# A hybrid attention and RWKV block: a PSUM set of its own for the first stage, five result places, three Newton steps

## The chip, the cores and the metric

The kernel runs on one core of a Trainium2 chip. The metric is the device time of one execution in microseconds (us). Five engines matter: PE (TensorE, matrix multiplication into the accumulator memory PSUM), DVE (VectorE), ACT (ScalarE), POOL (GpSimd) and SP, which issues nearly all transfers (DMA). Each engine runs its own instructions strictly in the order in which they stand, and waits for others through semaphores.

## What is computed

One layer of a sequence model on 1024 tokens with 16 learned tokens ahead of them (1040 columns), width 1024. Cut to what matters here:

```python
hn = rms_norm(h, norm_mix)                 # first stage, by columns
proj = hn @ w_in                           # q, k, v, f_logit, rw, gates
log_f = log_sigmoid(f_logit + f_b)
fcum = cumsum(log_f)                       # "forget": bias of the attention
z = rw + mu * (rw_prev - rw)               # token shift
r, kr, vr, zw, za, zg = split(z)
w_log = -softplus(-(w0 + tanh(zw) @ w_up)) - 0.5
a_rate = sigmoid(a0 + za @ a_up)           # low-rank products: w_up, a_up, g_up
g = sigmoid(zg) @ g_up
...                                        # attention, RWKV scan, gates, w_out
h = h + mixer(...)
h = h + conv_ffn(rms_norm(h, norm_ffn))    # feed-forward, the larger half of the time
```

## The kernel before

Every large product is made of three fp32r matmuls, high times high, high times low and low times high (lines 218, 219, 220), where `wh`, `wl` are the two parts of a weight and `xh`, `xl` those of the normalized input. A projection of one block of 128 output rows over one column chunk is 8 times 3 = 24 matmuls.

The first stage (`stage0`) goes over three column chunks, 0 to 384, 384 to 768, and 768 to 1040. In each, `stats` squares the input (ACT), adds (DVE) and takes column means on PE (line 624) in `rsqrt_rows`; there DVE makes an inverse root by Newton steps of three instructions each (lines 632 to 634), and PE spreads it over the partitions (line 639). `norm` multiplies it in (DVE, line 154, `xt`), rounds (ACT, line 156, `xh`) and takes the rest (line 158, `xl`, on POOL and DVE in turn). `lora` then makes two projections with token shift, `sg` and `wa` (24 matmuls each, evicted by ACT at line 268 and DVE at line 269), and from them twelve low-rank products (line 173): four times a trio of two on 64 rows from `wa` and one on 128 rows from `sg`. ACT evicts each product into a place `o` (lines 176 and 178), POOL scales one of three (line 180), and SP stores it (line 181) to `tha_d`, `sw_d` or `g_d`. The stage ends with the load of another ACT function table (line 191).

After it, several streams run side by side: `att` begins with `forget`, whose 48 matmuls (line 580) in three groups of 16 give the forget logits; a chain on ACT and DVE then makes their running sums, stores them to `f_d`, and POOL's queue loads them into `k2` (line 699) for the attention. `rec` begins with `prep`, which projects K, R and V for four pairs of heads (`zk`, `zr`, `zv`; `proj`, line 347; again 24 matmuls a chunk).

What order each engine has is not written by hand. All streams are recorded, and a scheduler that estimates times puts every engine's instructions into an order when the program is built. It knows the dependences, among them those that come from shared buffers: a PSUM accumulator can't be written before its earlier content is evicted, and a pool of PSUM can't be opened over space that another pool holds.

PSUM accumulators are named by a role, and a table gives the places that a role goes through in turn: A, B, t, o are single banks, S and M two banks each, used as two halves. In the first stage of before it reads:

```python
    banks(S, mm="S S M M", st="t o", pr="A B", t="t", o="o")
```

So projections of the first stage (role `mm`) use halves of S and M, statistics (`st`) use t and o, and the low-rank products use A and B, under the role `pr`, which `prep`'s projections have as well. The matmuls of `forget` use S and M again.

Of the kernel before, what the change touches and what calls it, by code (L numbers as in the profile page):

```python
# [14 lines left out]
PSUM = bass.MemoryType.PSUM  # L15
# [40 lines left out]
def constants(S):  # L56

    nc, A, cp = S.nc, S.A, S.cp
    par = cp.tile([P, NPAR], F32, name="par")
    nc.sync.dma_start(out=par[:], in_=A["par"])  # L60
    S.par = lambda name, i=0: par[:, _PCOLS[name][0] + i:_PCOLS[name][0] + i + 1]
    S.pr = lambda name: par[:, _PCOLS[name][0]:_PCOLS[name][0] + _PCOLS[name][1]]
    S.ident = cp.tile([P, P], F32, name="ident")
    nc.sync.dma_start(out=S.ident[:], in_=A["ident"])
    S.ones = cp.tile([P, P], F32, name="ones")
    nc.vector.memset(S.ones[:], 1.0 / D)
    S.eps = cp.tile([P, 1], F32, name="eps")
    nc.vector.memset(S.eps[:], NORM_EPS)
    S.geps = cp.tile([P, 1], F32, name="geps")
    nc.vector.memset(S.geps[:], GN_EPS)  # L70
    S.wc = cp.tile([P, NCH, 4], F32, name="wc")
# [31 lines left out]
def stage0(S):  # L103

    nc, tc = S.nc, S.tc
    S.xhi = {}
    S.xh = [S.xp.tile([P, L + 2], F32R, name="xh", tag="x") for _ in range(KD)]
    S.xl = [S.xp.tile([P, L + 2], F32R, name="xl", tag="x") for _ in range(KD)]
    for k in range(KD):
        nc.gpsimd.memset(S.xh[k][:, 0:2].bitcast(F32), 0.0)  # L110
        nc.gpsimd.memset(S.xl[k][:, 0:2].bitcast(F32), 0.0)
    with tc.tile_pool(name="s0", bufs=1) as p0:
        T = lambda name, bufs, tag=None: p0.tile([P, 384], F32, name=name, tag=tag or name, bufs=bufs)
        xs, w0 = [], []
        for c, (t0, t1) in enumerate(G):
            tl = [p0.tile([P, 2, 384], F32, name="xt", bufs=8) for _ in range(4)]
            for k in range(4):
                nc.sync.dma_start(out=tl[k][:, :, :t1 - t0], in_=S.A["xT"][:, 2 * k:2 * k + 2, t0:t1])
            xs.append([tl[k // 2][:, k % 2] for k in range(KD)])
            if c == 0:  # L120
                constants(S)
            if c < 2:
                w0.append(wload(S, S.A["w_rw"][c], KD, p0))
                u = p0.tile([P, 512], F32, name=("lup", "gup")[c])
                nc.sync.dma_start(out=u[:], in_=S.A[("lup", "gup")[c]])
                if c:
                    gup = u
                else:
                    lup = u
            if c == 1:  # L130
                constants2(S)

        def stats(c):

            n = G[c][1] - G[c][0]
            xt = xs[c]
            sq = []
            na = 2
            for k in range(KD):
                with tc.issue_after(S.xhi[k].ins) if c == 1 else nullcontext():  # L140
                    sq.append(T("sq", 4))
                    nc.scalar.activation(out=sq[k][:, :n], in_=xt[k][:, :n], func=AF.Square)
                    if k >= na:
                        nc.vector.tensor_tensor(out=sq[k % na][:, :n], in0=sq[k % na][:, :n], in1=sq[k][:, :n], op=ALU.add)
            ps = psum(S, "st")
            rsqrt_rows(S, p0, ps, sq[:na], n, S.ones[:, 0:1], 1, eps=NORM_EPS)
            return ps

        def norm(c, ps):
            t0, t1 = G[c]  # L150
            n = t1 - t0
            for k in range(KD):
                xt = xs[c][k]
                nc.vector.scalar_tensor_tensor(out=xt[:, :n], in0=xt[:, :n], scalar=S.par("norm_mix", k),
                                               in1=ps[:, :n], op0=ALU.mult, op1=ALU.mult)
                S.xhi[k] = nc.scalar.copy(out=S.xh[k][:, 2 + t0:2 + t1], in_=xt[:, :n])  # L156
                eng = nc.vector if k % 2 else nc.gpsimd
                eng.tensor_tensor(out=S.xl[k][:, 2 + t0:2 + t1], in0=xt[:, :n], in1=S.xh[k][:, 2 + t0:2 + t1], op=ALU.subtract)  # L158

        def lora(c):  # L160
            t0, t1 = G[c]
            n = t1 - t0
            sg, wa = T("sg", 1), T("wa", 1)
            rw_tile(S, 0, sg[:, :n], w0[0], c)
            nc.scalar.activation(out=sg[:, :n], in_=sg[:, :n], func=AF.Tanh, scale=0.5)
            nc.gpsimd.tensor_scalar(out=sg[:, :n], in0=sg[:, :n], scalar1=0.5, scalar2=0.5, op0=ALU.mult, op1=ALU.add)
            rw_tile(S, 1, wa[:, :n], w0[1], c)
            nc.scalar.activation(out=wa[0:64, :n], in_=wa[0:64, :n], func=AF.Tanh)
            for p in range(NP_):
                pc = slice(p * P, (p + 1) * P)  # L170
                for i, (l, r) in enumerate(((lup[0:64, pc], wa[0:64, :n]), (lup[64:128, pc], wa[64:128, :n]), (gup[:, pc], sg[:, :n]))):
                    ps = psum(S, "pr")
                    nc.tensor.matmul(ps[:, :n], lhsT=l, rhs=r, start=True, stop=True)
                    o = T("o", 3)
                    if i == 2:
                        nc.scalar.copy(out=o[:, :n], in_=ps[:, :n])
                    else:
                        S.tanh = nc.scalar.activation(out=o[:, :n], in_=ps[:, :n], func=AF.Tanh, scale=0.5, bias=(S.w0h, S.a0h)[i][:, p:p + 1])
                    if i == 0:
                        nc.gpsimd.tensor_scalar(out=o[:, :n], in0=o[:, :n], scalar1=0.5, scalar2=0.5, op0=ALU.mult, op1=ALU.add)  # L180
                    nc.sync.dma_start(out=(S.sw_d, S.tha_d, S.g_d)[i][p, :, t0:t1], in_=o[:, :n])

        ps = stats(0)
        norm(0, ps)
        lora(0)
        for c in (1, 2):
            ps = stats(c)
            norm(c, ps)
            lora(c)
    with tc.issue_after(S.tanh.ins):  # L190
        S.ld = nc.scalar.preload_act_table_set("natural_log_exp_and_others")
# [35 lines left out]
def banks(S, **use):  # L227

    S.psb.update({k: v.split() for k, v in use.items()})
    S.psn.update({k: 0 for k in use})  # L230
# [8 lines left out]
def psum(S, tag):  # L239

    slots = S.psb[tag]
    n = S.psn[tag] % len(slots)
    S.psn[tag] += 1
    t = slots[n]
    if n and slots[n - 1] == t:
        return S.half[tag][:, 512:1024]
    S.half[tag] = slot(S, t, tag)
    return S.half[tag][:, 0:512]
# [364 lines left out]
def rsqrt_rows(S, pool, ps, sq, n, ind, w, eps):  # L613


    nc = S.nc
    nb = -(-n // P)
    while n % nb:
        nb += 1
    m = n // nb  # L620
    o = 496
    for j in range(nb):
        for i, q in enumerate(sq):
            nc.tensor.matmul(ps[:m, o + w * j:o + w * j + w], lhsT=q[:, j * m:j * m + m], rhs=ind, start=i == 0, stop=i == len(sq) - 1)
    W = w * nb
    vt, yt, tt = [pool.tile([P, 8], F32, name=nm, bufs=2) for nm in ("rv", "ry", "rt")]
    v, y, t = vt[:m, :W], yt[:m, :W], tt[:m, :W]
    nc.vector.tensor_scalar(out=v, in0=ps[:m, o:o + W], scalar1=eps, scalar2=None, op0=ALU.add)

    nc.vector.tensor_scalar(out=y.bitcast(I32), in0=v.bitcast(I32), scalar1=-0.5, scalar2=1597463007.0, op0=ALU.mult, op1=ALU.add)  # L630
    for _ in range(4):
        nc.vector.tensor_tensor(out=t, in0=v, in1=y, op=ALU.mult)
        nc.vector.scalar_tensor_tensor(out=t, in0=t, scalar=-0.5, in1=y, op0=ALU.mult, op1=ALU.mult)
        nc.vector.scalar_tensor_tensor(out=y, in0=t, scalar=1.5, in1=y, op0=ALU.add, op1=ALU.mult)
    for j in range(nb):
        for i in range(w):
            r = P // w
            l = yt[:m, w * j + i:w * j + i + 1].broadcast_to([m, r])
            nc.tensor.matmul(ps[i * r:(i + 1) * r, j * m:(j + 1) * m], lhsT=l, rhs=S.ident[:m, :m], start=True, stop=True)
# [251 lines left out]
def stage12(S):  # L891

    nc, tc = S.nc, S.tc
    banks(S, mm="S S M M", st="t o", pr="A B", t="t", o="o")
    pq_cm = tc.tile_pool(name="ps1", bufs=1, space=PSUM)
    S.pq = pq_cm.__enter__()
    p1_cm = tc.tile_pool(name="p1", bufs=1, side="right")
    p1 = p1_cm.__enter__()
    S.smask = p1.tile([P, 384], BF16, name="smask")
    nc.gpsimd.memset(S.smask[:], 1.0)  # L900
    nc.gpsimd.memset(S.smask[:].rearrange("p (c t) -> p c t", t=64)[:, :, 0:1], 0.0)
    stage0(S)
    banks(S, mm="S M")
    S.op = S.rp = None
    S.scanned = False
    S.ev = 0
# [401 lines left out]
```

## Time and profile before

| | |
|---|---|
| time, three runs | 1931.68, 1933.45, 1941.54 us; median 1933.45 |
| profiled execution | 1933.08 us, its span 1930.9 us |
| mean granted TensorE clock | 0.969 |
| PE busy | 1815.3 us, 94% of the span |
| DVE, ACT, POOL busy | 58%, 40%, 40% |
| chain that ended last | PE 54%, DVE 4%, DMA 2%, ACT 2% |

Busy time is the time in which an engine had an instruction running, and the rest of the span is what it waited. The granted clock is the mean of what the chip gave TensorE, 1.00 being 2.4 GHz and 0.50 the lower of its two levels, 1.2 GHz. The chain follows the work that ended last back from the end.

### The profile page before, as it was taken

To read this page: it belongs to the slowest core of one execution; us is meant where nothing else is said; L and a number is where in the kernel's file an instruction comes from. 1 tells how busy PE (TensorE), PEld (TensorE's weight loads), DVE (VectorE), ACT (ScalarE), POOL (GpSimd) and SP (SyncE) were. 2 spreads that over 40 slices of the span, in tenths; PEclk is the share of its full clock that TensorE was granted. 3 is DMA by queue.
4 is the path that set the end of the run, shared out by engine and by line. 5 is a ranking of instruction groups with operands and counts; after the bars stand their busy time and mean duration, and the time that the engine had idled before them with its cause. 6 is when DMAs were issued, how large, how long until landed. Compare 5 with 4: busy or idle time off the path is not lost.

```text
span 1930.9 us, 33790 instructions
## 1 busy us (share of the span) xinstructions
PE 1815.3 (94%) x12744; PEld 1628.9 (84%) x12744; DVE 1114.6 (58%) x2062; ACT 770.8 (40%) x1706; POOL 766.7 (40%) x858
## 2 busy tenths in 40 slices
PE   6899999999998899999879998989999999999998
PEld 5588778788787688989769997979999899899996
DVE  6225635645727686442346447575756856757567
ACT  5345434444635432243365324333323333233232
POOL 4134224223324311232313334353744834636546
PEclk9899999899999899999989999999999999999998
DMA  5221331332413455565654332111121111211112
GB/s 183 95 71 44 83 77 55 79 88 57 112 47 90 95 138 154 156 188 160 188 147 137 111 123 84 36 53 44 44 67 44 44 46 43 66 44 44 61 39 104
DMA packets 197578, 170.84 MB, mean 88 GB/s; under 512 B 93768, under 2 KB 154744, under 8 KB 197416
## 3 DMA queue, kind: packets, MB, share of 16 engines
q1 hardware_dynamic: 197160, 168.62, 30.6%
q8 instruction: 101, 1.65, 0.4%
q14 instruction: 61, 0.50, 0.1%
q0 software_dynamic: 256, 0.07, 0.0%
HBM read 122.57 MB, written 46.06 MB: 87 GB/s over the span
## 4 chain that ended last, share of the span: by engine, by line
PE 54%; DVE 4%; DMA 2%; ACT 2%; issue 1%; POOL 1%; SPq 1%; DVEq 0%; ACTq 0%; POOLq 0%
PE mm L219 11%; PE mm L218 11%; PE mm L220 11%; PE dn L219 3%; PE dn L218 3%; PE dn L220 3%; PE gate L218 3%; PE gate L219 3%; PE gate L220 3%; DVE h L1171 1%; DMA y<-y_d 1%; DVE x L1041 1%; PE ch L541 1%; DVE x L1038 0%; PE ch L534 0%
## 5 line engine op out<-in xcount | busy, mean ns | idle before, releaser
L206 POOL TENSOR_TENSOR wl<-wf,wh 128x512 fp32r<-128x512 f32 x220 | 289.5, 1319 | 524.7 <-ACT wh L205 488.6
L218 PE MATMUL mm<-x,wh 128*128 128x344 f32 (+1 forms) x1056 | 338.3, 320 | 6.2 <-DVE ug L1139 6.2
L219 PE MATMUL mm<-x,wh 128*128 128x344 f32 (+1 forms) x1056 | 339.6, 322 | 0.0
L220 PE MATMUL mm<-x,wl 128*128 128x344 f32 (+1 forms) x1056 | 337.2, 320 | 1.0 <-POOL wl L206 1.0
L1171 DVE TENSOR_TENSOR h<-h,dn 128x512 f32<-128x512 f32 x288 | 183.3, 683 | 40.4 <-PE dn L220 32.8
L218 PEld LDWEIGHTS mm<-x,wh 128*128 128x128 f32 x1056 | 199.9, 189 | 7.1 <-ACT uv L1137 6.5
L205 ACT CAST wh<-wf 128x512 fp32r<-128x512 f32 x220 | 135.6, 617 | 164.8 <-PE mm L219 69.2
L220 PEld LDWEIGHTS mm<-x,wl 128*128 128x128 f32 x1056 | 199.4, 189 | 1.8 <-POOL wl L206 1.5
L219 PEld LDWEIGHTS mm<-x,wh 128*128 128x128 f32 x1056 | 200.0, 189 | 0.5
L218 PE MATMUL dn<-gx,wh 128*128 128x512 f32 x308 | 123.2, 401 | 11.1 <-ACT gx L1102 5.7
L218 PE MATMUL gate<-xh,wh 128*128 128x342 f32 x384 | 127.3, 332 | 4.1 <-ACT sg L856 2.1
L219 PE MATMUL gate<-xl,wh 128*128 128x342 f32 x384 | 127.3, 332 | 0.0
L220 PE MATMUL gate<-xh,wl 128*128 128x342 f32 x384 | 126.6, 330 | 0.0
L219 PE MATMUL dn<-gx,wh 128*128 128x512 f32 x308 | 122.6, 398 | 0.6 <-POOL gx L1103 0.6
L220 PE MATMUL dn<-gx,wl 128*128 128x512 f32 x308 | 122.1, 397 | 0.0
L218 PE MATMUL mm<-xh,wh 128*128 128x348 f32 (+5 forms) x336 | 116.9, 348 | 3.9 <-ACT xh L156 1.8
L219 PE MATMUL mm<-xl,wh 128*128 128x348 f32 (+5 forms) x336 | 114.4, 341 | 1.6 <-POOL xl L158 1.2
L220 PE MATMUL mm<-xh,wl 128*128 128x348 f32 (+5 forms) x336 | 112.6, 335 | 0.0
L1138 DVE SCALAR_TENSOR_TENSOR uv<-mm,par,uv 128x342 f32<-128x342 f32 (+1 forms) x66 | 37.7, 571 | 109.3 <-ACT uv L1137 109.3
L218 PE MATMUL pr<-xh,wh 128*128 128x386 f32 (+1 forms) x288 | 95.9, 333 | 1.4 <-ACT bt L469 1.4
L1084 POOL TENSOR_TENSOR wl<-ws,wh 128x256 fp32r<-128x256 f32 (+1 forms) x120 | 81.9, 694 | 33.5 <-ACT wh L1083 33.4
L219 PE MATMUL pr<-xl,wh 128*128 128x386 f32 (+1 forms) x288 | 94.8, 329 | 0.0
(317 smaller groups left out, 4333.1 us busy)
## 6 DMA issues: line engine op xcount, KB each, us to landing
wf<-in_w_up_dram SPq DMA_DIRECT2D x88, 256.0 KB, 2.7
wf<-in_w_down_dram SPq DMA_DIRECT2D x40, 256.0 KB, 2.8
sg_d<-sg SPq DMA_DIRECT2D x48, 171.0 KB, 3.4
sg<-sg_d SPq DMA_DIRECT2D x48, 171.0 KB, 2.4
wf<-in_w_gate_dram SPq DMA_DIRECT2D x32, 256.0 KB, 4.5
wf<-in_w_out_dram SPq DMA_DIRECT2D x32, 256.0 KB, 2.7
wf<-in_w_rw_dram SPq DMA_DIRECT2D x28, 256.0 KB, 2.8
wf<-in_w_qkv_dram SPq DMA_DIRECT2D x24, 256.0 KB, 2.8
```

The lines of the kernel that those rows point to most:

```text
L205: nc.scalar.copy(out=wh[:, :n], in_=wf[:, :n])
L206: nc.gpsimd.tensor_tensor(out=wl[:, :n], in0=wf[:, :n], in1=wh[:, :n], op=ALU.subtract)
L218: nc.tensor.matmul(ps, lhsT=wh, rhs=xh, start=first and k == 0, stop=False)
L219: nc.tensor.matmul(ps, lhsT=wh, rhs=xl, start=False, stop=False)
L220: nc.tensor.matmul(ps, lhsT=wl, rhs=xh, start=False, stop=last and k == n - 1)
L541: nc.tensor.matmul(pz[r, q, :], lhsT=bkt[:, q, r], rhs=uv[e][:, q, :], start=True, stop=True)
L1041: (nc.gpsimd if m in (3, 7) else nc.vector).tensor_tensor(out=l[:, s], in0=x[:], in1=h[:, s], op=ALU.subtract)
L1084: nc.gpsimd.tensor_tensor(out=wl[:, o], in0=x, in1=wh[:, o], op=ALU.subtract)
L1138: nc.vector.scalar_tensor_tensor(out=t[:, :n], in0=ps[:, 1:1 + n], scalar=cw(1), in1=t[:, :n], op0=ALU.mult, op1=ALU.add)
L1171: nc.vector.tensor_tensor(out=half(r, c), in0=half(r, c), in1=ps[:], op=ALU.add if sign > 0 else ALU.subtract)
```

## The change

The first stage gets accumulators of its own: single banks 0 and 1 for its projections, 2 and 3 for the low-rank products under a new role `lr`, in a pool `ps0` that is closed before the pool `ps1` with S and M is opened over the same space. Banks A and B are left to `prep`'s projections (`pr`). The results `o` get five places in SBUF in place of three. `rsqrt_rows`, which the first stage and the feed-forward stage call three times each, makes three Newton steps in place of four.

```diff
--- before.py
+++ after.py
@@ -169,9 +169,9 @@
             for p in range(NP_):
                 pc = slice(p * P, (p + 1) * P)
                 for i, (l, r) in enumerate(((lup[0:64, pc], wa[0:64, :n]), (lup[64:128, pc], wa[64:128, :n]), (gup[:, pc], sg[:, :n]))):
-                    ps = psum(S, "pr")
+                    ps = psum(S, "lr")
                     nc.tensor.matmul(ps[:, :n], lhsT=l, rhs=r, start=True, stop=True)
-                    o = T("o", 3)
+                    o = T("o", 5)
                     if i == 2:
                         nc.scalar.copy(out=o[:, :n], in_=ps[:, :n])
                     else:
@@ -628,7 +628,7 @@
     nc.vector.tensor_scalar(out=v, in0=ps[:m, o:o + W], scalar1=eps, scalar2=None, op0=ALU.add)
 
     nc.vector.tensor_scalar(out=y.bitcast(I32), in0=v.bitcast(I32), scalar1=-0.5, scalar2=1597463007.0, op0=ALU.mult, op1=ALU.add)
-    for _ in range(4):
+    for _ in range(3):
         nc.vector.tensor_tensor(out=t, in0=v, in1=y, op=ALU.mult)
         nc.vector.scalar_tensor_tensor(out=t, in0=t, scalar=-0.5, in1=y, op0=ALU.mult, op1=ALU.mult)
         nc.vector.scalar_tensor_tensor(out=y, in0=t, scalar=1.5, in1=y, op0=ALU.add, op1=ALU.mult)
@@ -891,16 +891,18 @@
 def stage12(S):
 
     nc, tc = S.nc, S.tc
-    banks(S, mm="S S M M", st="t o", pr="A B", t="t", o="o")
-    pq_cm = tc.tile_pool(name="ps1", bufs=1, space=PSUM)
-    S.pq = pq_cm.__enter__()
+
+    banks(S, mm="0 1", st="t o", lr="2 3", pr="A B")
     p1_cm = tc.tile_pool(name="p1", bufs=1, side="right")
     p1 = p1_cm.__enter__()
     S.smask = p1.tile([P, 384], BF16, name="smask")
     nc.gpsimd.memset(S.smask[:], 1.0)
     nc.gpsimd.memset(S.smask[:].rearrange("p (c t) -> p c t", t=64)[:, :, 0:1], 0.0)
-    stage0(S)
-    banks(S, mm="S M")
+    with tc.tile_pool(name="ps0", bufs=1, space=PSUM) as S.pq:
+        stage0(S)
+    pq_cm = tc.tile_pool(name="ps1", bufs=1, space=PSUM)
+    S.pq = pq_cm.__enter__()
+    banks(S, mm="S M", t="t", o="o")
     S.op = S.rp = None
     S.scanned = False
     S.ev = 0
```

The order of instructions changes as follows. The first place is PE at the beginning of the second column chunk. In before, once the first chunk's inverse root of chunk 1 is spread, low-rank products of chunk 0 (`pr<-wa` or `sg`) and one projection stand there; `mm_485` is that of `sg`, and the number at the end of an operand tells buffers apart.

```order
L639 MATMUL st_432<-ident_138,ry_440 128x128 x3
L173 MATMUL pr_352<-wa_289,lup_159 128x384
L173 MATMUL pr_346<-wa_289,lup_159 128x384
L218 MATMUL mm_485<-xh_93,wh_149 128x386
L173 MATMUL pr_357<-sg_288,gup_181 128x384
L219 MATMUL mm_485<-xl_101,wh_149 128x386
L220 MATMUL mm_485<-xh_93,wl_150 128x386
L218 MATMUL mm_485<-xh_94,wh_149 128x386
```

In the changed kernel three projections go side by side from there: `mm_480` is `sg`, `mm_509` is `wa`, and `pr_944` is the first K projection of `prep`.

```order
L173 MATMUL lr_360<-wa_286,lup_159 128x384
L173 MATMUL lr_366<-wa_286,lup_159 128x384
L218 MATMUL mm_480<-xh_93,wh_149 128x386
L218 MATMUL mm_509<-xh_93,wh_171 128x386
L218 MATMUL pr_944<-xh_93,wh_905 128x386
L173 MATMUL lr_371<-sg_285,gup_181 128x384
L219 MATMUL mm_480<-xl_101,wh_149 128x386
L220 MATMUL mm_480<-xh_93,wl_150 128x386
L218 MATMUL mm_480<-xh_94,wh_149 128x386
L219 MATMUL mm_509<-xl_101,wh_171 128x386
```

Here `wa`'s group, which in before comes after the chunk-2 group of `sg`, and a group of `prep`, which in before comes after the whole first stage, moved up between the low-rank products. The same is done in the other chunks: by the end of the first stage the changed kernel has made the first K projection in all three chunks and the first 12 of 24 matmuls in each of the first two chunks of the R projection (`pr_1070`, `pr_1163`).

The second place is PE near the end of the first stage. In before, the last of the first group of 16 forget matmuls is followed by the rest of the low-rank products of chunk 1, and the `wa` group of chunk 2 (`mm_683`).

```order
L580 MATMUL mm_840<-xl_108,wfh_810 40x348
L173 MATMUL pr_541<-wa_484,lup_159 128x384
L173 MATMUL pr_552<-sg_483,gup_181 128x384
L173 MATMUL pr_557<-wa_484,lup_159 128x384
L173 MATMUL pr_563<-wa_484,lup_159 128x384
L173 MATMUL pr_568<-sg_483,gup_181 128x384
L173 MATMUL pr_573<-wa_484,lup_159 128x384
L173 MATMUL pr_579<-wa_484,lup_159 128x384
L173 MATMUL pr_584<-sg_483,gup_181 128x384
L173 MATMUL pr_589<-wa_484,lup_159 128x384
L173 MATMUL pr_595<-wa_484,lup_159 128x384
L173 MATMUL pr_600<-sg_483,gup_181 128x384
```

In the changed kernel the low-rank products of chunk 2 (`lr<-wa_675`, `sg_674`) stand in one row, and behind them the forget matmuls (`mm_819`), all 48 together.

```order
L173 MATMUL lr_744<-sg_674,gup_181 128x272
L173 MATMUL lr_749<-wa_675,lup_159 128x272
L173 MATMUL lr_755<-wa_675,lup_159 128x272
L173 MATMUL lr_760<-sg_674,gup_181 128x272
L173 MATMUL lr_765<-wa_675,lup_159 128x272
L173 MATMUL lr_771<-wa_675,lup_159 128x272
L173 MATMUL lr_776<-sg_674,gup_181 128x272
L173 MATMUL lr_781<-wa_675,lup_159 128x272
L173 MATMUL lr_787<-wa_675,lup_159 128x272
L173 MATMUL lr_792<-sg_674,gup_181 128x272
L580 MATMUL mm_819<-xh_93,wfh_808 40x348
L580 MATMUL mm_819<-xl_101,wfh_808 40x348
```

The forget matmuls moved behind all low-rank products, since their place lies over `ps0`.

The third place is ACT at the same end. In before the table load (line 191) stands ahead of the last eviction of a low-rank product, and then come forget's evictions (line 582).

```order
L176 COPY o_784<-pr_782 128x272
L178 ACTIVATE o_789<-pr_787,lin_w0_185 128x272
L178 ACTIVATE o_795<-pr_793,lin_a0_187 128x272
L191 ACT_TABLE_LOAD
L176 COPY o_800<-pr_798 128x272
L582 ACTIVATE fl_814<-mm_821,par_136 8x348
L582 ACTIVATE fl_814<-mm_840,par_136 8x348
```

In the changed kernel two exponentials of `prep` (lines 380 and 381) stand there as well.

```order
L178 ACTIVATE o_783<-lr_781,lin_w0_185 128x272
L178 ACTIVATE o_789<-lr_787,lin_a0_187 128x272
L191 ACT_TABLE_LOAD
L380 ACTIVATE ex_1627<-cs_1620 128x6x64
L381 ACTIVATE ei_1628<-cs_1620 128x384
L176 COPY o_794<-lr_792 128x272
L582 ACTIVATE fl_812<-mm_819,par_136 8x348
L583 COPY l_813<-mm_819 8x348
```

So between the last two evictions of low-rank products there are now the table load and two exponentials, and the first forget matmul waits for the last of these evictions.

Behind the first stage the order on each engine is that of before again, but for a few neighbours. On POOL two weight splits (line 206) that stood behind the loads of `k2` stand ahead of them. In the feed-forward stage the matmuls of line 639 stand a few rows earlier, the last of its three groups by four matmuls.

## Rows read from the trace of the kernel before

**Rows 1.** Windows: length, busy PE, PEld, DVE, ACT, POOL, granted clock, DMA share, GB/s
```profile
20.00:40.00 20.00, 17.59 (x76) 15.95 (x77) 15.56 (x34) 11.10 (x26) 8.60 (x9) 0.83 0.42 124
40.00:60.00 20.00, 19.08 (x88) 12.92 (x89) 17.04 (x41) 13.79 (x32) 10.19 (x13) 1.00 0.39 138
60.00:80.00 20.00, 14.82 (x56) 8.58 (x54) 0.62 (x1) 4.75 (x10) 1.41 (x4) 0.86 0.25 80
80.00:100.00 20.00, 16.52 (x58) 10.16 (x58) 1.00 (x2) 5.67 (x13) 1.87 (x4) 0.72 0.19 70
100.00:120.00 20.00, 17.76 (x76) 14.30 (x76) 1.18 (x2) 10.09 (x20) 6.35 (x16) 0.83 0.24 81
```

**Rows 2.** Timeline of PE, first column chunk
```profile
18.22 0.66 PE L218 MATMUL mm<-xh,wh 128*128 128x386 f32 x1 [1.62 <-ACT xh L156]
...
30.14 2.77 PE L624 MATMUL st<-ones,sq 128*128 128x1 f32 x12 [2.08 <-DVE sq L144]
32.76 0.67 PE L218 MATMUL mm<-xh,wh 128*128 128x386 f32 x1
...
36.77 0.35 PE L218 MATMUL mm<-xh,wh 128*128 128x386 f32 x1
```

**Rows 3.** Timeline of PE, a group at the higher clock level: first and last
```profile
59.77 0.34 PE L218 MATMUL mm<-xh,wh 128*128 128x386 f32 x1
...
63.82 0.34 PE L220 MATMUL mm<-xh,wl 128*128 128x386 f32 x1
```

**Rows 4.** Timeline of PE, low-rank products of chunks 1 and 2
```profile
70.73 0.88 PE L173 MATMUL pr<-sg,gup 128*128 128x384 f32 x2 [0.81 <-ACT o L178]
71.54 1.55 PE L173 MATMUL pr<-wa,lup 64*128 64x384 f32 x4
75.15 1.65 PE L173 MATMUL pr<-sg,gup 128*128 128x384 f32 x2 [2.06 <-ACT o L178]
...
93.47 0.72 PE L173 MATMUL pr<-wa,lup 64*128 64x272 f32 x2 [1.11 <-DVE wa L269]
...
98.20 0.70 PE L173 MATMUL pr<-sg,gup 128*128 128x272 f32 x2 [0.67 <-ACT o L178]
98.83 1.27 PE L173 MATMUL pr<-wa,lup 64*128 64x272 f32 x4
```

**Rows 5.** Timeline of PE, the last group of forget matmuls, and what follows it
```profile
116.52 0.32 PE L580 MATMUL mm<-xh,wfh 128*40 128x344 f32 x1
...
119.06 0.34 PE L218 MATMUL pr<-xh,wh 128*128 128x386 f32 x1
```

**Rows 6.** Timeline of ACT, end of the first stage
```profile
74.52 0.58 ACT L178 ACTIVATE o<-pr,lin_w 128x384 f32<-128x384 f32 x1 [2.39 <-DMA tha_d<-o]
...
107.21 1.28 ACT L191 ACT_TABLE_LOAD   x1
108.51 0.39 ACT L176 COPY o<-pr 128x272 f32<-128x272 f32 x1
...
116.28 0.51 ACT L381 ACTIVATE ei<-cs 128x384 f32<-128x384 f32 x1
```

**Rows 7.** Waits from 60 to 120 us: total us, times, longest us
```profile
PE pr L173 <- ACT o L178: 6.9, 7, 2.1
```

**Rows 8.** Timeline of DVE, last Newton step of the first chunk
```profile
14.54 0.16 DVE L633 SCALAR_TENSOR_TENSOR rt<-rt,ry 128x3 f32<-128x3 f32 x1
14.74 0.16 DVE L634 SCALAR_TENSOR_TENSOR ry<-rt,ry 128x3 f32<-128x3 f32 x1
```

**Rows 9.** Timeline of PE in the feed-forward stage
```profile
1196.33 0.82 PE L639 MATMUL st<-ident,ry 114*128 114x114 f32 x6
...
1207.19 0.63 PE L218 MATMUL mm<-x,wh 128*128 128x344 f32 x1 [6.25 <-DVE ug L1139]
```

**Rows 10.** Timeline of POOL: the load of the forget sums, a later weight split
```profile
134.91 1.26 POOL L699 DMA_DIRECT2D k<-f_d  x2
...
150.95 1.29 POOL L206 TENSOR_TENSOR wl<-wf,wh 128x512 fp32r<-128x512 f32 x1 [9.00 <-ACT wh L205]
```

## The prediction

> **What bounds the kernel now.** I began with the page's shares: PE is busy for 94% of the span and leads the chain that ended last, so only time in which PE waits or runs at the lower clock can be won. Windows of 20 us show where that is [rows 1]. From 20 to 40 us PE is busy 17.59 of 20 at a mean granted clock of 0.83, from 40 to 60 it is nearly full (19.08, clock 1.00), and from 60 to 120 it is busy 14.82, 16.52 and 17.76 at 0.86, 0.72 and 0.83. In that last stretch DVE works about 1 us in 20 and ACT 5 to 10, so no engine is the bound there: PE waits in a ring. The waits name it: PE waits 6.9 us for ACT to evict low-rank products [rows 7], and ACT for the store of an earlier result, 2.39 us in one case [rows 6]. With three places, a trio of results waits for the trio before it to land. After such a wait of 2.06 us the product on 128 rows takes 1.65 us where it took 0.88 before [rows 4], which is the lower clock level.
>
> How much is lost? PE's first projection begins at 18.22 [rows 2], and the forget matmuls end at 119.06 [rows 5]: 100.8 us. The work in it at the higher level:
> - a group of 24 matmuls on 386 columns: 4.05 us between the starts of its first and last [rows 3], over 23 steps 0.176 each. 96 of them make 16.9, and 48 on 274 columns, scaled by the columns (an estimate, 0.125), 6.0.
> - low-rank products: a trio of chunks 0 and 1 is 0.81 (from 70.73 to the next start) and 1.55, 2.36 in all; one of chunk 2 is 0.63 and 1.27, 1.90 in all [rows 4]. Eight and four trios: 18.9 and 7.6.
> - forget: 16 matmuls from 116.52 to 119.06, 2.54 [rows 5], three times 7.6.
> - of `prep`, in the order of before, 39 matmuls: 6.9.
> - statistics of two chunks: a group of line 624 is 2.62 us at the lower level (30.14 to 32.76, rows 2), half of it 1.3; a group of line 639 is 0.82 [rows 9]. Together 4.2.
>
> The sum is 68.1, so 32.7 us of the 100.8 are lost: to waits, and to the lower clock behind them.
>
> **The change, part by part.** *Newton steps.* Three DVE instructions go at 0.20 us each [rows 8], 0.6 us per call. In chunk 0 PE waits for it at the start: its first projection begins at 17.6. In chunks 1 and 2 PE has other work meanwhile: 0. In the feed-forward stage the last spread at 1196.33 [rows 9] stands in PE's order, and moves ahead of four matmuls of 0.16: 0.6 us. DVE's normalization waits for that, and PE then idles 6.25 us for DVE [rows 9], so it counts in full.
>
> *Own PSUM.* `prep`'s first groups run inside the first stage. In work that is, beyond the 39 matmuls above, 9 of K in chunk 1, 24 of chunk 2, and 24 of the R projection: 33 times 0.176 and 24 times 0.125, 8.8 us. So when the changed kernel ends its forget matmuls it stands where before stood 8.8 us after 119.06, at 127.9. The table below takes its time from 17.6.
>
> 1. Chunk 0, 48 projection matmuls of `sg` and `wa` side by side: 8.4 us of work. In before, `sg`'s 24 took from 18.22 to 28.06 (30.14 less 2.08 of waiting, rows 2), 9.8 where 4.2 would do: 5.6 lost to pieces of `xl` that come late and to the lower clock. A second group fills the waits but needs the same pieces, and the clock may stay low. The bounds are 0 and 5.6; I take 4.4.
> 2. The 2.08 us wait for the chunk-1 squares [rows 2] goes: a K group stands there now.
> 3. All work until the chunk-2 products, 77.0 less 8.4, less 7.6 for them, less 7.6 for forget (where 77.0 is 68.1 and 8.8): 53.3 us. Every low-rank product there has matmuls of other groups behind it, so its eviction is hidden, as in before from 40 to 60 us, where PE is idle 0.92 of 20 [rows 1]. At that rate 2.5 are lost. If the new groups leave no wait it is 0; if DVE, busy 17.04 of 20 from 40 to 60, makes `xl` too late, perhaps 5.
> 4. Before the chunk-2 products PE must wait for `wa` to be evicted and for its tanh; in before that was 1.11 [rows 4]. I take 1.3.
> 5. Twelve products in one row on two banks. Nothing else is behind them. ACT needs 0.39 to 0.58 for an eviction [rows 6], a product 0.63, and with two banks a product and its eviction may take two products' time. Five places cover the landing: an `o` comes back after 5 products, over 3 us, where the longest wait of before was 2.39 for the landing with three. I add 0.7 to the 7.6. Bounds: 0, and the lower clock throughout, another 7.6.
> 6. Ahead of the last eviction ACT loads its table, 1.28, and runs two exponentials of 0.51 less overlap, then evicts in 0.39 [rows 6]: PE has nothing to do for 2.7 us. In before this load hid behind a K group, and that cover is gone since the group is done.
> 7. Behind that wait I expect the lower clock, as behind the 2.08 and 2.06 above. In before it lasted from 30.14 until the matmuls shorten to 0.35 at 36.77 [rows 2], 6.6 us. That costs half, 3.3. Bounds: 0 and 3.8 (all 7.6 us of forget at half speed). Forget's own evictions wait for all stores to land, which 5.1 us of two matmul groups hide.
>
> Sum: 17.6 + 77.0 + 4.4 + 2.5 + 1.3 + 0.7 + 2.7 + 3.3 = 109.5, against 127.9: 18.4 us won. With the feed-forward stage it is 19.0, from the profiled execution's own 1933.08 to 1914.1. The median of the runs, 1933.45, lies 0.4 above it, so I say **1914**.
>
> *Five places alone* are worth nothing elsewhere. They take effect in step 5 and under the groups of step 3.
>
> **The rivals.**
> - *Better.* The clock stays up in steps 1 and 7 and step 3 loses nothing: 4.4, 3.3 and 2.5 more, 10.2, so 1904. Against it: both waits of 2 us that the rows of before show dropped the clock.
> - *The tail at half clock.* Each product of step 5 leaves a short wait, and PE alternates over two banks. If that keeps the clock at the lower level, the twelve cost 7.6 more: 1921.5. For it: from 80 to 100 us the clock was 0.72 [rows 1]. Against it: products at 98.20 and 98.83, after a wait of 0.67, are at the higher level [rows 4]. The Trainium skill ("TensorE: Matmul & The Clock Gate", "A second HAM failure mode: psum-queue depth-cycling") says that short idles between groups that cycle through PSUM banks can make the clock swing, which speaks for this rival. The trace of before has the low level after waits of 2 us and not after this one of 0.67.
> - *Given back later.* Forget ends only 119.06 less 109.5, 9.6 us earlier, but the rest of PE's work 18.4. The loads of `k2` stand on POOL's queue at 134.91, 15.9 after forget; now that is 125.4. Behind them is a weight split that ran at 150.95 [rows 10] and is needed at 132.5 now. After issue (1.26) and split (1.29) it is ready at 128.0, 4.5 us to spare, and two earlier splits have moved ahead of the loads. If the sums are later by more than 4.5, PE waits for each further us. To bring the gain under 0.5% (9.7) they would have to be 14 late: about 1925 to 1933.
> - *The other side: slow clock through the mixed groups.* In step 3 three groups interleaved on late pieces of `xl` could stop PE again and again, so that it never leaves the lower level. All of the 53 us at half speed would cost 53; the gain is gone when 19 us of that work run at half, and it is slower by 0.5% at 29: 1933 to 1960. Against it: in before one group and low-rank products, mixed in the same way, ran from 40 to 60 at clock 1.00 with both DVE and ACT busy [rows 1], and now there is more to fill a wait with.
>
> **How the numbers follow.** The forecast (1908 to 1919) has a chance of 0.62, the better case 0.11, the tail at half clock (1919 to 1924) 0.12, given back 0.09, the slow clock 0.06. The range is to reach to the bounds of steps 1, 3, 5 and 7, from 1904 to 1923; it leaves out the last two cases and the ends of others, somewhat under 0.2. A difference under 0.5%, 9.7 us, is about what a measurement here can't tell from none; 1923.8 is that bound. Faster: 0.85, from the first three cases. Same 0.09, slower 0.06.
>
> **What the profile of the changed kernel would show.** PE's first projection near 17.6; the group of line 624 for chunk 1 with no wait of 2 us; 40 to 84 us nearly full at clock 1.00; the last twelve low-rank products within some 8.5 us, without a wait for a store; a PE wait of 2 to 3 us with the last eviction as its releaser; 48 forget matmuls in 8 to 11 us, ending near 109.5; and all work from there to about 1150 us earlier by 18 us. Forget ending after 118 would show step 3 or 5 wrong, and an early end without an earlier feed-forward stage would show the gain given back.

## The result, and the profile after

| | before | changed |
|---|---|---|
| median of six runs each | 1936.8 us | 1916.53 us |
| range | 1931.68 to 1943.78 | 1912.37 to 1920.50 |
| ratio, 95% interval | | 0.990 (0.9879 to 0.9921) |
| profiled execution, its span | 1933.08, 1930.9 | 1917.22, 1915.3 |

The change is worth 20.3 us by the medians, a gain of 0.8 to 1.2% by the interval, and 15.9 us between the two profiled executions. Runs of one kernel differ by 8 to 12 us here, so a single profile tells an end time no better than that; what happens in the first stage is much steadier, as the experiments show.

The windows of the changed kernel that answer to [rows 1] (length, busy us of PE, PEld, DVE, ACT, POOL, granted clock, DMA share, GB/s):

```profile
20.00:40.00 20.00, 19.58 (x109) 17.31 (x108) 16.56 (x34) 13.80 (x32) 10.37 (x10) 1.00 0.47 141
40.00:60.00 20.00, 20.00 (x97) 15.36 (x96) 12.24 (x30) 11.01 (x25) 7.94 (x8) 1.00 0.38 132
60.00:80.00 20.00, 19.84 (x115) 15.59 (x114) 5.99 (x13) 9.30 (x21) 7.89 (x12) 1.00 0.38 130
80.00:100.00 20.00, 16.68 (x42) 8.22 (x42) 1.00 (x2) 10.59 (x22) 4.22 (x9) 0.65 0.37 128
100.00:120.00 20.00, 20.00 (x113) 17.41 (x112) 8.45 (x12) 7.04 (x16) 5.96 (x13) 0.92 0.05 14
```

From 20 to 80 us PE now has work nearly all the time (19.58, 20.00 and 19.84 of 20), and the windows give a granted clock of 1.00. They don't show one thing: up to 24.40 the matmuls start 0.32 us apart, twice the 0.18 behind it, as at the lower level. What is left of the old picture is from 80 to 100 us: 16.68 busy at a clock of 0.65.

The timeline of PE in the changed kernel answers to [rows 2, 4, 5 and 9]:

```profile
18.42 0.98 PE L218 MATMUL mm<-xh,wh 128*128 128x386 f32 x2 [1.34 <-ACT xh L156]
...
24.08 0.53 PE L218 MATMUL mm<-xh,wh 128*128 128x386 f32 x1
...
24.90 0.34 PE L218 MATMUL mm<-xh,wh 128*128 128x386 f32 x1
...
30.58 0.34 PE L218 MATMUL pr<-xh,wh 128*128 128x386 f32 x1
...
31.52 1.24 PE L624 MATMUL st<-ones,sq 128*128 128x1 f32 x10
...
84.41 1.33 PE L173 MATMUL lr<-wa,lup 64*128 64x272 f32 x4 [0.66 <-ACT o L176]
86.46 1.25 PE L173 MATMUL lr<-sg,gup 128*128 128x272 f32 x2 [0.72 <-ACT o L178]
87.64 1.81 PE L173 MATMUL lr<-wa,lup 64*128 64x272 f32 x4
...
95.64 1.27 PE L173 MATMUL lr<-sg,gup 128*128 128x272 f32 x2
98.75 0.51 PE L580 MATMUL mm<-xh,wfh 128*40 128x348 f32 x1 [1.83 <-ACT o L176]
...
108.42 0.34 PE L218 MATMUL mm<-xh,wh 128*128 128x384 f32 x1
...
1189.47 0.63 PE L218 MATMUL mm<-x,wh 128*128 128x344 f32 x1 [5.62 <-DVE ug L1141]
```

The reader sees the first projection at 18.42, the first K group of `prep` at 30.58, line 624 without the wait of 2.08 us, then the row of twelve low-rank products of chunk 2 from 84.41 to 96.91, forget's matmuls from 98.75 to 108.42, and far below the feed-forward stage, where PE's wait for DVE is 5.62 in place of 6.25. In the row of products the first pair, behind a wait of 0.66, takes 1.33. Behind the second wait, of 0.72, every pair takes 1.81 to 1.86 and every product of `sg` some 1.27: the lower level. That second wait is for ACT's first eviction of the row, which begins 1.4 us after the first product, since ACT works on `sg` and `wa` until then:

```profile
85.83 0.49 ACT L178 ACTIVATE o<-lr,lin_w 128x272 f32<-128x272 f32 x1
```

Waits of PE from 60 to 115 us:

```profile
PE mm L580 <- ACT o L176: 1.8, 1, 1.8
PE lr L173 <- ACT o L178: 0.9, 2, 0.7
PE lr L173 <- ACT o L176: 0.7, 1, 0.7
```

The 6.9 us of [rows 7] are 1.6 now.

A place that all the kernels below have in common is the first matmul of line 386, in `prep`, where the first stage's gain has become visible in full: in every one of them PE has 775 recorded matmuls ahead of it. The view of that line in the changed kernel (count, duration of the shortest, median and longest, first and last start):

```profile
L386 PE MATMUL pr<-kk,bo x24: 392/485/590, 165.9 to 626.6; 128*128 128x384 f32 x16, 128*128 128x272 f32 x8
```

In before it is 185.4, so 19.5 us are won there. The twenty equal windows between the start and this point show how: PE's waits fall from 29.2 to 18.1 us, and the time at the lower clock level (window length times twice what the clock lacks to 1) from 30.8 to 17.1, half of which is lost. That is 11.1 and 6.9 of the 19.5.

### The profile page after: what moved, and what is told of

The parts are those of the page before. It is cut to its first block, busy times and chain, and to the rows that moved or that the text cites. A ratio compares the mean times of both kernels' runs of the same rounds, so it can differ in the third digit from the quotient of the medians.

```text
span 1915.3 us, 33775 instructions
## 1 busy us (share of the span) xinstructions
PE 1812.8 (95%) x12744; PEld 1628.6 (85%) x12744; DVE 1112.5 (58%) x2044; ACT 770.9 (40%) x1706; POOL 769.5 (40%) x858
## 3 DMA queue, kind: packets, MB, share of 16 engines
q1 hardware_dynamic: 197160, 168.62, 30.8%
## 4 chain that ended last, share of the span: by engine, by line
PE 55%; DMA 3%; DVE 2%; POOL 2%; ACT 2%; issue 1%; SPq 1%; POOLq 0%; ACTq 0%; DVEq 0%
PE mm L219 11%; PE mm L218 11%; PE mm L220 11%; PE dn L218 4%; PE dn L219 4%; PE dn L220 4%; PE gate L219 3%; PE gate L218 3%; PE gate L220 2%; DMA y<-y_d 1%; POOL wl L206 1%; PE ch L541 1%; PE ch L534 0%; DMA y_d<-yt 0%; PE ch L523 0%
## 5 line engine op out<-in xcount | busy, mean ns | idle before, releaser
L1078 POOL TENSOR_TENSOR ws<-wf 128x256 f32<-128x256 f32 (+1 forms) x120 | 85.5, 720 | 22.0 <-DMA wf<-in_w_down_dram 20.2
```

The costliest lines, as they stand in the source:

```text
L1078: nc.gpsimd.tensor_tensor(out=t[:, :n], in0=x, in1=y, op=op)
```

## Experiments

All were timed beside the kernel before. Its median was 1938.17, 1936.83 and 1935.03 in the three batches (first e1 to e4; then a2 and e5 to e7; last e8 to e11), so ratios are the better guide. *First 386* is the first matmul of line 386. *Middle* is the time from there to the first addition of squares in the feed-forward stage (line 1060, in the changed kernel 1062, in e7 1065). Both are from one profile of each kernel. *Old order* says whether PE's instructions, behind the first stage and up to row 2000 of its order, stand as in before but for a few neighbours, that is, in attention and the RWKV preparation.

| kernel | median us | ratio, interval | first 386 | middle | old order |
|---|---|---|---|---|---|
| before | see text | 1 | 185.4 | 912.7 | yes |
| changed | 1916.53 | 0.990 (0.9879 to 0.9921) | 165.9 | 916.6 | yes |
| a2, changed again | 1914.56 | 0.9886 (0.9857 to 0.9914) | 164.8 | 912.7 | yes |
| e1, five places alone | 1933.18 | 0.9971 (0.9959 to 0.9982) | 177.2 | 921.3 | no |
| e2, three steps alone | 1931.30 | 0.9966 (0.9951 to 0.998) | 185.3 | 906.4 | no |
| e3, PSUM set alone | 1920.72 | 0.9906 (0.9881 to 0.9932) | 166.3 | 922.9 | no |
| e4, PSUM set, three steps | 1921.45 | 0.9912 (0.9898 to 0.9927) | 166.2 | 922.7 | no |
| e5, four banks at the end | 1914.55 | 0.9882 (0.9854 to 0.991) | 159.0 | 912.6 | yes |
| e6, table load last | 1923.52 | 0.9936 (0.9912 to 0.9959) | 164.1 | 926.0 | no |
| e7, forget early | 1923.66 | 0.9932 (0.9909 to 0.9954) | 167.3 | 919.4 | no |
| e8, products on A and B | 1922.25 | 0.9928 (0.991 to 0.9946) | 167.7 | 921.1 | no |
| e9, one projection bank | 1921.48 | 0.9922 (0.9904 to 0.994) | 173.6 | 913.6 | yes |
| e10, four banks, six places | 1910.12 | 0.9872 (0.9855 to 0.989) | 159.7 | 916.2 | yes |
| e11, e5 again | 1912.26 | 0.9885 (0.9863 to 0.9906) | 161.3 | 917.2 | yes |

### The three parts alone

**e1.** The kernel before, with

```diff
-                    o = T("o", 3)
+                    o = T("o", 5)
```

> The kernel before with five result places and nothing else. If the own PSUM set makes the gain (theory), the waits for stores go but the low-rank products of the later chunks still have no other matmuls behind them: 2 to 7 us faster than before, the stretch 64 to 107 us shortened by that. If the places make it (rival), 10 to 19 us faster.

Measured: 0.9971, 5 us. At line 386 it is 8.2 us ahead. PE's waits for ACT from 60 to 120 us fell from the 6.9 of [rows 7] to 3.1 (1.4 and, for line 176, 1.7), but over the first stage they fall only from 29.2 to 26.6. The larger part is clock: the time at the lower level before line 386 falls from 30.8 to 13.7 us, and half of the difference is 8.5. The middle then takes 8.6 us longer and gives it back in the profile. The rival falls.

**e2.** The kernel before, with

```diff
-    for _ in range(4):
+    for _ in range(3):
```

> The kernel before with three Newton steps and nothing else. Theory: 0.6 us in chunk 0 and 0.6 us in the feed-forward stage, about 1 us faster, no difference that the runs can tell. Rival (the new order that the scheduler makes of it is worth more): over 4 us either way.

Measured: 0.9966, some 6.9 us, which the theory had not expected. None of it comes from the first stage (185.3 against 185.4). The middle takes 6.3 us less. The windows from 200 to 400 us, in e2 first, then in before:

```profile
200.00:300.00 100.00, 95.81 (x781) 80.28 (x782) 47.72 (x116) 40.09 (x107) 23.15 (x33) 1.00 0.34 85
300.00:400.00 100.00, 91.84 (x738) 74.92 (x737) 70.21 (x157) 54.22 (x142) 33.53 (x41) 1.00 0.32 80
```

```profile
200.00:300.00 100.00, 93.88 (x773) 78.89 (x772) 46.95 (x118) 40.24 (x108) 22.51 (x33) 0.96 0.34 85
300.00:400.00 100.00, 91.89 (x653) 76.22 (x652) 65.06 (x141) 53.79 (x139) 32.27 (x38) 0.90 0.29 74
```

PE waits somewhat less in e2 (4.2 and 8.2 us against 6.1 and 8.1), and the clock stays up there, where before has 0.96 and 0.90. So the rival of this run was right: a small edit in the first stage comes with another order 200 us later, and the runs with that order are several us faster.

**e3 and e4.** The PSUM set as in the changed kernel, with three places and four steps (e3), and with three places and three steps (e4, whose first stage has the same order as the changed kernel on every engine).

> The kernel before with the first stage's own PSUM set, three places and four steps. Theory: 14 to 19 us faster than before, the forget matmuls end within 5 us of the changed kernel's 108.5. Rival (the places are needed with it, as the stores come back too late in the row of twelve products): 5 to 12 us faster, with waits of ACT for stores over 1 us in that row.

> The changed kernel with three result places in place of five; the order of the first stage is the same on every engine. Theory: a trio of the last chunk took 3.1 us in the changed kernel, at the lower clock, as long as a store's round trip, so the places are worth 0 to 2 us: within 2 us of the changed kernel. Rival (the places matter): the row of twelve products takes 16 us or more in place of 12.5, and the time is 3 to 6 us above the changed kernel's.

Measured: at line 386 both are where the changed kernel is (166.3 and 166.2 against 165.9). So the PSUM set makes nearly all that the first stage wins. Counted from the first projection, which takes out when the first means arrive, line 386 comes 148.6 us later in e4 and 147.5 and 147.6 in the changed kernel and a2, so by these profiles the places are worth some 1 us there; on the old banks, in e1, they were worth 8. The timeline of PE in the row of twelve products in e4 shows one wait more, for a store behind ACT, and the row takes 13.2 us in place of 12.5:

```profile
86.04 0.97 PE L173 MATMUL lr<-sg,gup 128*128 128x272 f32 x2 [0.72 <-ACT o L178]
...
89.91 1.28 PE L173 MATMUL lr<-sg,gup 128*128 128x272 f32 x2 [1.15 <-ACT o L178]
```

By the medians both end 4 to 5 us above the changed kernel, by the ratios 1 to 2 (and 4 to 5 above a2); the intervals meet, so a difference at the end is likely and not shown. In the profiles their middle takes 6 us longer, with an order other than before's. The theory for e3 (14 to 19 us faster) came true with 17.4; that for e4 (within 2 us) missed by the medians, on account of the middle.

The Newton step shows where statistics arrive. On DVE of e3 (four steps) and e4 (three), line 628 takes the column means and line 154 begins to normalize:

```profile
11.90 0.16 DVE L628 TENSOR_SCALAR rv<-st 128x3 f32<-128x3 f32 x1 [2.39 <-PE st L624]
16.68 3.76 DVE L154 SCALAR_TENSOR_TENSOR xt<-xt,par,st 128x384 f32<-128x384 f32 x7 [1.74 <-PE st L639]
```

```profile
12.09 0.16 DVE L628 TENSOR_SCALAR rv<-st 128x3 f32<-128x3 f32 x1 [2.39 <-PE st L624]
16.29 4.29 DVE L154 SCALAR_TENSOR_TENSOR xt<-xt,par,st 128x384 f32<-128x384 f32 x8 [1.75 <-PE st L639]
```

4.78 and 4.20: 0.58 us for three instructions. In the feed-forward stage PE's wait of [rows 9] is 6.2 or 6.3 in the three kernels with four steps (before, e1, e3) and 5.6 in all others.

### What follows the groups: four banks, table load, forget

**a2** is the changed kernel again.

> The changed kernel once more, as the base for the three that follow. Theory: the 19 us won by 186 us into the run are kept until 640 us, since the order of instructions there is that of before; 17 to 22 us faster than before.

22.3 us faster, just above the range, 20.6 of them won by line 386; the same waits of 0.66 and 0.72 and the same slow row.

**e5, e11, e10.** In the changed kernel the products of the last chunk go through four banks, as the projections' two are free by then. e10 has six result places as well.

```diff
-            nc.scalar.activation(out=wa[0:64, :n], in_=wa[0:64, :n], func=AF.Tanh)
+            nc.scalar.activation(out=wa[0:64, :n], in_=wa[0:64, :n], func=AF.Tanh); banks(S, lr="2 3 0 1" if c == 2 else "2 3")
```

> The changed kernel with the twelve products of chunk 2 on four banks in place of two, since the projections' banks are free then; the order is the same on every engine. Theory (the waits for evictions bring the clock down): no wait between products, the clock stays up, and the row takes 8 to 9 us in place of 12.5, so 3 to 6 us faster than the changed kernel. Rival (a row of such products runs at the lower clock for another reason): the row stays over 11 us with the waits gone, 0 to 1.5 us faster.

> e5 once more, for a second profile and more times. Theory: the row of products at the higher clock again, 6.5 to 7.5 us. Rival (chance): over 10 us. For the time: 2 to 6 us below the changed kernel's median of 1915 to 1917 if the first stage's gain is kept, 0 if the later stage eats it.

> Four banks in the last chunk as in e5, and six result places in place of five; the order is that of the changed kernel. Theory (four banks let the row of products run at full clock): the row takes 6.5 to 7.5 us again and forget's matmuls end near 101, 6 us before the changed kernel's; store waits of 0.7 us in e5 go. The median 0 to 6 us below the changed kernel's. Rival (the clock in e5's profile was chance): the row takes over 10 us.

The timeline of PE in e5 in the same row of products:

```profile
83.95 1.79 PE L173 MATMUL lr<-wa,lup 64*128 64x272 f32 x6 [0.66 <-ACT o L176]
85.87 0.72 PE L173 MATMUL lr<-sg,gup 128*128 128x272 f32 x2
86.53 0.72 PE L173 MATMUL lr<-wa,lup 64*128 64x272 f32 x2
...
87.83 0.73 PE L173 MATMUL lr<-wa,lup 64*128 64x272 f32 x4
...
90.07 0.73 PE L173 MATMUL lr<-sg,gup 128*128 128x272 f32 x2
93.90 0.35 PE L580 MATMUL mm<-xh,wfh 128*40 128x348 f32 x1 [3.10 <-ACT o L176]
```

Of the two waits only the first is left. Every product is at the higher level, and the row takes 6.85 us (83.95 to 90.80) in place of 12.5. It is so in all three profiles (6.5 us in e10, 7.1 in e11), so that it was no chance. Not all of it is clock. At 87.83 two products on 64 rows each run at the same time, in 0.73 us together. In e1, on two banks and at the higher level, such a pair takes 1.27, and ten products follow each other without a wait between them:

```profile
94.85 0.70 PE L173 MATMUL pr<-sg,gup 128*128 128x272 f32 x2 [0.67 <-ACT o L178]
95.48 1.27 PE L173 MATMUL pr<-wa,lup 64*128 64x272 f32 x4
```

At the pace of e1, 6.48 us for ten, twelve would take 7.8 (an estimate). So of the 5.7 us some 0.9 are this overlap, 0.7 the wait, and about 4 the clock. At line 386 they stand 3.5 to 7 us ahead of the changed kernel and a2. PE then waits 3.1 us for ACT, as the row ends before ACT has loaded its table. In e5 the clock stays up after that wait (0.35 and 0.32 per matmul from 93.90); in e10 and e11 it doesn't:

```profile
89.42 0.73 PE L173 MATMUL lr<-sg,gup 128*128 128x272 f32 x2
93.18 0.51 PE L580 MATMUL mm<-xh,wfh 128*40 128x348 f32 x1 [3.03 <-ACT o L176]
```

Forget's matmuls end at 101.55, 102.23 and 103.87 in e5, e10 and e11, where 108.42 is the changed kernel's. By the medians e5 is equal to a2 in its batch, where 3 to 6 us were expected, and e11 and e10 are the fastest of theirs, with e10 0.9872 the lowest of all. Its interval meets those of a2 and the changed kernel, so that the version is faster at the end is likely and not shown; that the row is faster is shown.

**e6.** The table load waits for the last eviction in place of the last tanh.

```diff
-                        nc.scalar.copy(out=o[:, :n], in_=ps[:, :n])
+                        S.last = nc.scalar.copy(out=o[:, :n], in_=ps[:, :n])
...
-    with tc.issue_after(S.tanh.ins):
+    with tc.issue_after(S.last.ins):
```

> The changed kernel with the ACT table load put behind the last eviction of the first stage in place of behind the last tanh. The order in the first stage is otherwise the same. Theory: PE's wait ahead of forget's matmuls, 1.8 us in the profile and 1.8 us between the last product's end and the first forget matmul, falls under 0.8 us; 1 to 2.5 us faster at that place; what is left of it at the end depends on the later order, which differs. Rival (the wait is for the pool's change of hands, not for the load): unchanged.

The wait ahead of forget, in the waits of PE:

```profile
PE mm L580 <- ACT o L176: 0.5, 1, 0.5
```

So it was the load, and not the pool's change of hands. The first stage is as good as any with two banks (164.1). The middle takes 926.0, the longest of all, and by the medians the kernel is 9 us slower than a2.

**e7.** Forget's matmuls on banks 0 and 1, inside the first stage's pool.

```diff
     with tc.tile_pool(name="ps0", bufs=1, space=PSUM) as S.pq:
         stage0(S)
+        a_cm = tc.tile_pool(name="a", bufs=1)
+        ap = a_cm.__enter__()
+        forget(S, ap)
...
-        with tc.tile_pool(name="a", bufs=1) as ap:
-            forget(S, ap)
+        if True:
...
+        a_cm.__exit__(None, None, None)
```

> The changed kernel with forget's matmuls on the first stage's projection banks 0 and 1 in place of S and M, so that they need not wait for the last eviction; two of three groups now stand between the last products. Theory: the row of products loses its waits in part, the 1.8 us wait ahead of forget goes, and the last forget matmul ends near 103 in place of 108.5, 4 to 6 us earlier; at the end as much, if the later order loses nothing. Rival (that stretch is hidden later anyway): the same time as the changed kernel though forget ends earlier.

It missed, in the first stage and at the end (by the medians 9 us slower than a2). The third group waits for a bank, that for ACT's eviction, and that for POOL to clear the target (line 574), which stands behind line 396 of `prep`. PE, ACT and POOL in turn:

```profile
104.39 0.51 PE L580 MATMUL mm<-xh,wfh 128*40 128x344 f32 x1 [6.38 <-ACT l L583]
```

```profile
102.78 1.09 ACT L582 ACTIVATE fl<-mm,par 8x348 f32<-8x348 f32 x2 [2.44 <-POOL fl L574]
```

```profile
100.15 2.05 POOL L396 TENSOR_TENSOR bk<-kf,ei 64x384 f32<-64x384 f32 x2 [0.24 <-ACT ei L381]
102.36 0.39 POOL L574 MEMSET fl<- 128x348 f32 x1 [0.15 <-POOL bk L396]
```

A wait of 6.38 us takes the place of the 1.83, and forget's last matmul ends at 108.7, no earlier than without the edit.

### What fills PE: e8 and e9

**e8** has the low-rank products on A and B again, so that the K and R groups can't go between them:

```diff
-    banks(S, mm="0 1", st="t o", lr="2 3", pr="A B")
+    banks(S, mm="0 1", st="t o", lr="A B", pr="A B")
```

> The changed kernel with the low-rank products on A and B again, so that they share those banks with the K and R projections as in before, while the first stage's projections keep banks 0 and 1. Theory (the gain comes from the K and R groups that fill PE's waits): most of it goes; the K groups stand behind all low-rank products again, and at the first wait of the attention (186 us in before) it is 4 to 9 us earlier than before in place of 19. Rival (single banks for the first stage's own projections are enough, as sg and wa go side by side): 15 to 20 us earlier.

This went against the theory. It is 17.7 us ahead at line 386 without any K or R group between the products. Its windows:

```profile
20.00:40.00 20.00, 17.35 (x68) 12.24 (x67) 15.63 (x31) 13.02 (x31) 9.85 (x10) 0.79 0.51 155
40.00:60.00 20.00, 20.00 (x87) 15.45 (x88) 10.49 (x24) 8.70 (x18) 5.63 (x7) 0.78 0.31 108
60.00:84.00 24.00, 22.45 (x106) 13.96 (x105) 7.93 (x16) 13.08 (x31) 6.44 (x12) 1.00 0.39 137
84.00:100.00 16.00, 15.92 (x75) 11.85 (x75) 1.18 (x2) 9.24 (x18) 4.14 (x13) 1.00 0.29 97
```

Since only projections lie in `ps0` now, that pool closes early, and forget's 48 matmuls fill the row of products, PE 15.92 of 16 busy at clock 1.00. From 20 to 60 us it loses more to the clock (0.79 and 0.78).

**e9** lets K and R groups between, but has one bank for `sg` and `wa`:

```diff
-    banks(S, mm="0 1", st="t o", lr="2 3", pr="A B")
+    banks(S, mm="0", st="t o", lr="2 3", pr="A B")
```

> The changed kernel with one bank for the first stage's projections in place of two, so that sg and wa can't go side by side, and the K and R groups can still go between. Theory: the K and R groups alone fill nearly all waits, 16 to 20 us earlier than before at the first wait of the attention. Rival (side by side is the larger part): 8 to 14 us.

It is 11.8 us ahead at line 386, within the rival's 8 to 14. The timeline of PE, the two groups of chunk 2:

```profile
87.69 0.60 PE L218 MATMUL mm<-xh,wh 128*128 128x274 f32 x1 [1.59 <-DVE sg L269]
...
93.52 1.19 PE L173 MATMUL lr<-wa,lup 64*128 64x272 f32 x4 [1.11 <-DVE wa L269]
```

With one bank `wa` waits for the eviction of `sg`, and the products wait for `wa`: 1.59 and 1.11. Before has both waits, the 1.11 in [rows 4] and the other in its own timeline, so there the two halves of one accumulator cost what one bank costs here:

```profile
87.20 0.60 PE L218 MATMUL mm<-xh,wh 128*128 128x274 f32 x1 [1.55 <-DVE sg L269]
```

## Why the prediction came out right

The forecast was 1914; by the median it is 1916.53, 2.5 us above it. Against the table of steps, from the changed kernel's timeline:

- **The start**, 17.6 forecast, 18.42 measured. The Newton step gave its 0.58 us, but the means on which it starts arrived at 12.92 in this execution and at 11.87 in before. In the fourteen profiles that arrival lies between 11.7 and 13.4, more than the step is worth.
- **Step 1**, 48 matmuls in 12.8: 12.2 (18.42 to 30.58). The matmuls go at the pace of the lower level up to 24.40, half of the step.
- **Step 2**: the wait of 2.08 is gone.
- **Step 3**, 53.3 and 2.5 lost: 53.2 (30.58 to 83.76), next to nothing lost. The term was an over-estimate of 2.6, since three groups side by side leave a single wait of 0.17.
- **Step 4**, 1.3: 0.66 and 0.72.
- **Step 5** is the step that failed: the row of products takes 11.8 beside the wait of 0.72, where 8.3 were forecast. The rival of the tail at half clock came true in this part, at 3.5 us more than forecast in place of its 7.6: the clock fell after waits of 0.66 and 0.72 and stayed down to the row's end, in the changed kernel, a2, e4 and e6; in e3 and e9 it fell a trio later, so six times in the six profiles that have this row whole on two banks, and in none of the three with four banks. The prediction held against this rival that before has a wait of 0.67 with products at the higher level behind it [rows 4]. That is so, but it read the row only that far: the same row of before goes on, with waits of 0.72 and 1.14, and ends at the lower level, a pair in 1.82:

```profile
103.87 0.73 PE L173 MATMUL pr<-sg,gup 128*128 128x272 f32 x2 [1.14 <-ACT o L178]
104.53 1.82 PE L173 MATMUL pr<-wa,lup 64*128 64x272 f32 x4
```

  Two banks alone don't bring the clock down: in e1, e7 and e8 the last eight to ten products run on two banks at the higher level, one behind the other without a wait of note. The fourteen profiles divide by the waits (products that forget's matmuls set apart not counted): all eight rows with two or more of 0.66 us or longer came to the lower level, and none of the six with at most one. The Trainium skill ("TensorE: Matmul & The Clock Gate", "A second HAM failure mode: psum-queue depth-cycling") describes a kernel whose short idles between groups of matmuls, with PSUM banks gone through in turn, make the clock swing. As to the idles the trace agrees, with a mean granted clock of 0.53 in a2 from 84 to 100 us and 1.00 in e5, where the second wait is gone.
- **Step 6**, 2.7: 1.83, since at the lower clock the last product itself covers part of the table load. With four banks it is 3.1.
- **Step 7**, 10.9: 9.67 (98.75 to 108.42).
- **The sum**, 109.5: 108.42, and so 19.5 won where 18.4 were forecast. Steps 1, 3, 6 and 7 were too high by some 5.3, step 5 and the start too low by 4.3, so that the sum is this close is in part luck.
- **The feed-forward stage**, 0.6: 0.63 (6.25 to 5.62).
- **Five places** were given a part in steps 3 and 5. With two banks it is some 1 us, by e4, which has three.

"Own PSUM" was the right part and its account was too narrow. The prediction's step 3 hides evictions and waits behind K and R groups. e8 shows that these are not needed, and e9 that they are not enough: what is needed is that `sg`, `wa` and the products can each go on without another's eviction, and then whatever is at hand fills PE. In before `sg` and `wa` were two halves of one accumulator; whether two halves that don't wait for each other would do with the old banks wasn't tried.

"Given back later" was given 0.09 and didn't happen. The loads of `k2` stand on POOL's queue where the prediction put them (125.4 forecast), and the split behind them waits for ACT, so that they held nothing up. The timeline of POOL in the changed kernel:

```profile
124.42 1.26 POOL L699 DMA_DIRECT2D k<-f_d  x2
131.40 1.29 POOL L206 TENSOR_TENSOR wl<-wf,wh 128x512 fp32r<-128x512 f32 x1 [5.72 <-ACT wh L205]
```

The profiled execution does give back 3.9 us in the middle (916.6 against 912.7), which is why its end is only 15.9 us earlier; a2, the same kernel, gives back none.

How much is kept goes with the order behind the first stage, which in the changed kernel is that of before. The seven kernels with that order have a middle of 912.6 to 917.2 us. Six with another have 919.4 to 926.0, and e2 906.4. So by these profiles the order there is worth some 6 us more or less, and so is the changed kernel's lead over e4 in the profiles. A good part of it is clock: time at the lower level in the middle, from twenty equal windows, is 59 us in e2, 71 to 80 in the kernels with the old order (68 in e9), 79 to 93 in the other six. e8, with 79, is no different in this from the old order. What in those orders brings the clock down stays open.

## What to carry to other kernels

Accumulators that two steps share, or halves of one, tie the steps together even where their data don't; ahead of a stage whose engines all wait in turn, look at which accumulator each of them waits for. Give a row of small products enough banks to go on while the engine that evicts them is still at other work: here an eviction (0.39 to 0.49) is shorter than a product (0.65), and two banks do once ACT keeps up (e1, e7, e8), but its first eviction came 1.4 us late. The short waits cost less than the clock that falls behind them. Where a scheduler writes the order, compare orders before crediting an edit: here an edit of 0.6 us came with an order worth 6.

## What the runs showed of the hardware that was not expected

- PE waits of 0.66 and 0.72 us within three us, in a row of products, were followed by the lower clock level for 17 us in the changed kernel (until forget was under way). All eight rows with two or more waits of 0.66 us or longer came to it (in before, e2 and e3 behind the third), and none of the six with at most one, three of them on two banks and three on four. A wait of 3.1 us was followed by it in e10 and e11, and not in e5, which is the same kernel as e11.
- On four banks, pairs of products on 64 rows each ran at the same time, 0.73 us for both (e5, e10, e11); on two banks a pair took 1.27 (e1). Both are at the higher level.
- Executions of one kernel spread over 4 to 17 us, those of before over 10 to 18 in a batch (a2: 1906.09 to 1920.11), without any difference in order. The arrival of the first means alone spreads over 1.7 us.
